# The long convolution of a hybrid encoder rewritten from radix four to radix eight

## The chip, the cores and the metric

The kernel is one program on one core of a Trainium2 chip, all in fp32 (the matmuls work on high and low parts, see below). The metric is the device time of one launch in microseconds (us), as the median of several runs. The engines have the names of the profile: PE is TensorE (PEld its weight loads), DVE is VectorE, ACT is ScalarE, POOL is GpSimd, SP is SyncE, which issues most DMAs.

## What is computed

Two encoder layers over 1024 tokens of width 1024. Each layer has token mixing, a cross-attention and a mixture of experts. Token mixing is a grouped-query attention, a long convolution ("hyena") of 256 channels and a latent attention, joined by one output projection. The change touches the convolution alone:

```python
def bidir_long_conv(z, h, bias):
    n_tok, c = z.shape[1], z.shape[2]
    hf, hb = h[:, 0], h[:, 1]
    filt_circ = jnp.concatenate([hf, jnp.zeros((1, c), jnp.float32), hb[1:][::-1]], axis=0)
    zf = z.astype(jnp.float32)
    zs = jnp.fft.rfft(zf, n=2 * n_tok, axis=1)
    fs = jnp.fft.rfft(filt_circ, axis=0)
    y = jnp.fft.irfft(zs * fs[None], n=2 * n_tok, axis=1)[:, :n_tok]
    return (y + zf * bias.astype(jnp.float32)).astype(z.dtype)

    # in hybrid_mix
    filt = hyena_filters(n_tok, hy_w1, hy_b1, hy_w2, hy_b2, hy_w3, hy_b3, hy_wout, hy_freq, hy_decay)
    out_b = x0 * bidir_long_conv(hv * x1, filt, hy_bias)
```

The filter h is the output of a small network (f3 in the kernel) times a decaying exponential, a window; it does not depend on x, and both layers' filters are transformed at the start of the program.

## The kernel before

**Transforms.** A transform of length 2048 with odd frequencies is split by the token index modulo four. Each of the four residues r has 256 tokens and a cosine and a sine table of 256 x 256. mm3 multiplies two operands that are each split in a high and a low part by three matmuls (L185 to L187); split (L173, L174) makes the two parts, the high one on ACT, the low one on DVE or POOL. dft_step does one residue: per kind (cosine, sine), per half of the frequencies and per half of the tokens an mm3 over 256 channels, 24 matmuls of 256 columns, the table stationary. evac (L179, L181) copies the result out of PSUM, on DVE and ACT in turn. Sums and differences of the residues ("butterflies") then give the spectrum F.

**filter_spectra** works both layers in three parts. First, per residue and layer, two windows: two matmuls (L868, L869), a product on DVE (L871), the sum and the difference of both halves on POOL (L875, L876), a split into pmh (ACT) and pml (DVE). Second, twelve dft_steps (the odd residues twice, since there sum and difference need both tables). Third, the butterflies (L916) and radix (L929), each one on DVE or POOL in turn by alt(); SP writes F to DRAM (fd). It is a generator, "fill": each next(fill) issues it up to its next yield. Two yields are taken in an earlier loop, 20 in the loop `for n in range(20)` (here the **filter loop**), beside the transposes of x and the projection's first tiles, and 22 in the **latent loop** of in_proj: for each of eight token tiles, 24 matmuls of 416 columns into one of two PSUM buffers (psO), with up to four next(fill) among them, and after them the tile's normalisation on ACT (square, root) and DVE (L371, L373, rotary L500 to L508), which frees the buffer.

**hyena(l)** is a generator as well. side() pulls it once per iteration of the attention, in iterations 3 to 57 except where n % 5 == 4 (44 pulls), and drains it at 58; one pull more comes before. It transposes z (L956), makes the four residues' transforms, does all butterflies on POOL, multiplies Z with F on POOL (L978 to L984), does the butterflies of the inverse on POOL (L990) and DVE (ab, L1004 to L1010), splits each ab (abh on ACT, abl on POOL) and transforms back with the spectrum stationary and the table moving. L1029 (DVE) adds the bias term from PSUM, into a buffer "yz", and L1033 (POOL) multiplies with the gate into mix.

**Attention** runs 96 iterations a layer, two to a head pair, of which the scores S (L524), the row maximum (DVE, L527), the exponential E (ACT, L533), four transposes (L541), the split of the probabilities (ACT PH, DVE PL) and the product with V (L551, L552) form a pipeline three iterations deep; S, T and O have two PSUM buffers each. After each pair put() moves the output: three copies on ACT (L563 to L565) into "olo", two instructions on POOL (L566, L567). olo and yz share one ring of two buffers:

```python
lo = self.tp.tile([128, 3, 256], F32, tag="olo", name="olo", bufs=2)       # put
t = self.tp.tile([128, 3, 256], F32, tag="olo", name="yz", bufs=2)[:, 0]   # hyena
```

**Order.** PE, ACT and DVE run in the order of the code; POOL's and SP's order is set by a scheduler at build time.

Of the kernel before, what the change touches and what calls it, by code (L numbers as in the profile page):

```python
# [19 lines left out]
D = 1024  # L20
# [47 lines left out]


# [14 lines left out]
def shape_constants():  # L84
# [10 lines left out]
    perm = np.concatenate([np.arange(r, N, 4) for r in range(4)])  # L95
# [6 lines left out]
    m, k = np.arange(256), np.arange(256)  # L102
    fwd, inv = [], []
    for r in range(4):
        th = np.pi * np.outer(4 * m + r, 2 * k + 1) / 2048
        cs = np.stack([np.cos(th), np.sin(th)], 1)
        fwd.append(cs.reshape(2, 128, 2, 256).transpose(1, 0, 2, 3).reshape(128, 1024))
        ci = (cs / 1024).transpose(2, 1, 0)
        inv.append(ci.reshape(2, 128, 2, 256).transpose(1, 0, 2, 3).reshape(128, 1024))
    for nm, v in (("k_dft", fwd), ("k_idft", inv)):  # L110
        v = np.stack(v).astype(np.float32)
        h = (v.view(np.uint32) + np.uint32(0x7FF) + ((v.view(np.uint32) >> np.uint32(12)) & np.uint32(1))) & np.uint32(0xFFFFF000)
        h = h.view(np.float32)
        out[nm] = np.stack([h, v - h], 1)
# [21 lines left out]
class Net:  # L136
# [661 lines left out]
    def table(self, name, r):  # L798
        res = []
        for i in range(2):  # L800
            t = self.big((128, 2, 2, 256), F32R, name="tab")
            self.nc.gpsimd.dma_start(t, self.A[name][r, i].rearrange("p (m c k) -> p m c k", m=2, c=2))
            res.append(t)
        return res

    def dft_step(self, r, tabs, cH, cL, sH, sL, free=False):

        nc = self.nc
        th, tl = tabs
# [6 lines left out]
        X = self.big((128, 2, 2, 256), name="X")  # L816
        if free:
            nc.scalar.activation(X, P, AF.Copy)
        else:
            self.evac(X, P)  # L820
        return X

# [4 lines left out]
    def filter_spectra(self):  # L827
# [13 lines left out]
        nc.sync.dma_start(tneg, A["k_tneg"])  # L841
        nxt = [self.table("k_dft", 0)]
# [4 lines left out]
        for w in ws:  # L847
            hl = self.big((128, 2, 512), F32R, name="woh")
            self.split(hl[:, 0], hl[:, 1], w)
            wp.append(hl)  # L850
        es, ends = {}, []

        def decay(j):
            if j < 8:
                r, l = divmod(j, 2)
                es[j] = []
                for i in (r * 2, r * 2 + 1):
                    e = self.tmp(name="win")
                    nc.scalar.activation(e, decs[l], AF.Exp, scale=tneg[:, i:i + 1])
                    es[j].append(e)  # L860

        def window(j, H, L):
            r, l = divmod(j, 2)
            a = slice(l * 64, l * 64 + 64)
            for mt in range(2):
                i = r * 2 + mt
                P, c = self.psO(), slice(i * 128, i * 128 + 128)
                nc.tensor.matmul(P, self.f3[l][:, c], wp[l][:, 0], start=True, stop=False)  # L868
                nc.tensor.matmul(P, self.f3[l][a, c], wp[l][a, 1], start=False, stop=True)  # L869
                e = es[j][mt]  # L870
                nc.vector.tensor_tensor(e, e, P, OP.mult)  # L871
                if i == 0:
                    nc.vector.memset(e[0:1, 256:512], 0.0)
                pm = self.tmp((128, 2, 256), name="pm")
                nc.gpsimd.tensor_tensor(pm[:, 0], e[:, 0:256], e[:, 256:512], OP.add)  # L875
                nc.gpsimd.tensor_tensor(pm[:, 1], e[:, 0:256], e[:, 256:512], OP.subtract)  # L876
                ends.append((H[:, :, mt, :], L[:, :, mt, :], pm))
            del es[j]

        def parts(n):  # L880
            for _ in range(n):
                self.split(*ends.pop(0))

        decay(0)
        yield
        G, H = [[], []], [{}, {}]
        for r in range(5):
            pms = []
            for l in range(DEPTH):
                if r < 4:  # L890
                    pmh = self.big((128, 2, 2, 256), F32R, name="pmh")
                    pml = self.big((128, 2, 2, 256), F32R, name="pml")
                    window(r * 2 + l, pmh, pml)
                    parts(len(ends) - 2)
                    decay(r * 2 + l + 1)
                    pms.append(((pmh[:, 0], pml[:, 0]), (pmh[:, 1], pml[:, 1])))
                    yield
                elif l == 0:
                    parts(2)
                if r > 0:  # L900
                    p, m = was[l]
                    G[l].append(self.dft_step(r - 1, tabs, *p, *m))
                    yield
                    if r % 2 == 0:
# [1032 lines left out]
```

## Time and profile before

| what | value |
|---|---|
| runs | 2755.35, 2754.78, 2750.19 us, median 2754.78 |
| profiled execution | 2756.29 us, span 2754.4 us |
| busy share of the span | PE 93%, PEld 79%, DVE 71%, ACT 57%, POOL 29% |
| chain that ended last | PE 72%, DVE 14%, ACT 5%, issue 5%, DMA 3%, POOL 1% |

The span is what the profiler sees of the execution; the rest of its time lies around it. Busy shares are means over the whole program, in which the convolution is a small part, so the stretches in which its pieces run have to be read by themselves: the filter loop at 83 to 143 us, the latent loop at 143 to 184, and two attentions, of which the first layer's has its iterations 15 to 48 at 422 to 517. In a row, `L916 POOL ... bf<-X 128x1024 x2` is two instructions of line 916 on POOL that make tile bf from tile X, 128 partitions by 1024 elements; the bracket at the end is the idle time of the engine before it and what ended that.

### The profile page before, as it was taken

To read this page: it belongs to the slowest core of one execution; us is meant where nothing else is said; L and a number is where in the kernel's file an instruction comes from. 1 tells how busy PE (TensorE), PEld (TensorE's weight loads), DVE (VectorE), ACT (ScalarE), POOL (GpSimd) and SP (SyncE) were. 2 spreads that over 40 slices of the span, in tenths; PEclk is the share of its full clock that TensorE was granted. 3 is DMA by queue.
4 is the path that set the end of the run, shared out by engine and by line. 5 is a ranking of instruction groups with operands and counts; after the bars stand their busy time and mean duration, and the time that the engine had idled before them with its cause. 6 is when DMAs were issued, how large, how long until landed. Compare 5 with 4: busy or idle time off the path is not lost.

```text
span 2754.4 us, 39814 instructions
## 1 busy us (share of the span) xinstructions
PE 2570.7 (93%) x14484; PEld 2175.1 (79%) x14484; DVE 1952.1 (71%) x3041; ACT 1577.6 (57%) x2804; POOL 810.4 (29%) x767
## 2 busy tenths in 40 slices
PE   7999989999999995999989999999999999599997
PEld 5788879888778884777869887988977888477775
DVE  6765568877653578889876556887765347888887
ACT  4633359878313443888854425887842344378885
POOL 3443427742201301111131333684230130011112
PEclk9999999999999997999999999999999999799999
DMA  7546110233232357999975611034223234799994
GB/s 194 183 163 206 40 47 32 93 100 96 81 99 86 104 180 256 348 378 371 342 238 170 211 62 47 24 100 100 72 90 107 77 101 175 248 329 371 378 345 153
DMA packets 224565, 468.04 MB, mean 170 GB/s; under 512 B 27001, under 2 KB 83919, under 8 KB 224368
## 3 DMA queue, kind: packets, MB, share of 16 engines
q1 hardware_dynamic: 197504, 369.32, 38.5%
q0 software_dynamic: 22256, 79.40, 10.4%
q10 hardware_dynamic: 4608, 16.78, 1.5%
q8 instruction: 114, 1.87, 0.3%
q14 instruction: 83, 0.68, 0.1%
HBM read 378.66 MB, written 86.77 MB: 169 GB/s over the span
## 4 chain that ended last, share of the span: by engine, by line
PE 72%; DVE 14%; ACT 5%; issue 5%; DMA 3%; POOL 1%; SPq 0%; ACTq 0%; DVEq 0%; POOLq 0%
PE S L185 8%; PE S L186 8%; PE S L187 7%; PE S L524 6%; PE O L1614 6%; PE T L541 5%; PE O L185 5%; PE O L186 5%; PE O L187 5%; PE S L418 4%; PE O L552 3%; PE O L551 3%; DVE rk L1417 1%; PE T L1368 1%; DMA ed<-moe_w_down 1%
## 5 line engine op out<-in xcount | busy, mean ns | idle before, releaser
L174 DVE TENSOR_TENSOR egl<-eg,egh 128x1024 fp32r<-128x1024 f32 x256 | 305.6, 1220 | 49.6 <-ACT egh L173 45.3
L527 DVE TENSOR_REDUCE nm<-S 128x1 f32<-128x1024 f32 x192 | 234.1, 1221 | 97.1 <-PE S L524 96.2
L173 ACT ACTIVATE egh<-eg 128x1024 fp32r<-128x1024 f32 x256 | 265.1, 1058 | 40.3 <-PE S L186 23.5
L174 DVE TENSOR_TENSOR PL<-T,PH 128x512 fp32r<-128x512 f32 x384 | 246.1, 682 | 17.3 <-ACT PH L173 15.0
L173 ACT ACTIVATE PH<-T 128x512 fp32r<-128x512 f32 x384 | 210.1, 595 | 81.7 <-PE T L541 80.4
L533 ACT ACTIVATE E<-S,nm 128x1024 f32<-128x1024 f32 x192 | 214.7, 1118 | 11.5 <-DVE nm L527 9.9
L185 PE MATMUL S<-woh,mh 128*128 128x512 f32 x512 | 207.8, 406 | 6.3 <-DVE r L1106 6.3
L541 PE MATMUL T<-ident,E 128*128 128x128 f32 x1536 | 206.1, 276 | 6.1 <-DVE PL L174 5.1
L541 PEld LDWEIGHTS T<-ident,E 128*128 128x128 f32 x1536 | 179.6, 142 | 40.1 <-DVE PL L174 14.6
L186 PE MATMUL S<-wol,mh 128*128 128x512 f32 x512 | 201.8, 394 | 2.8 <-POOL wol L174 2.4
L185 PE MATMUL S<-egh,xt 128*128 128x512 f32 x512 | 203.9, 398 | 0.0
L187 PE MATMUL S<-woh,ml 128*128 128x512 f32 x512 | 200.8, 392 | 0.0
L187 PE MATMUL S<-egh,xt 128*128 128x512 f32 x512 | 200.4, 391 | 0.0
L186 PE MATMUL S<-egl,xt 128*128 128x512 f32 x512 | 200.4, 391 | 0.0
L174 DVE TENSOR_TENSOR edl<-ed,edh 128x1024 fp32r<-128x1024 f32 x128 | 153.1, 1220 | 18.5 <-ACT edh L173 18.5
L1614 PE MATMUL O<-edh,ht 128*128 128x512 f32 x512 | 156.2, 408 | 1.4 <-ACT ht L173 1.4
L566 POOL TENSOR_TENSOR olo<-olo 64x256 f32<-64x256 f32 x96 | 70.2, 731 | 293.3 <-ACT olo L564 289.4
L524 PE MATMUL S<-KS,QS 128*128 128x512 f32 x512 | 148.2, 413 | 2.4 <-ACT E L533 2.4
L173 ACT ACTIVATE edh<-ed 128x1024 fp32r<-128x1024 f32 x128 | 132.4, 1055 | 22.9 <-PE S L186 13.2
L1556 POOL DMA_INDIRECT xg<-x2d,ix x32 | 54.9, 1715 | 299.2 <-PE O L1614 124.3
L551 PE MATMUL O<-PH,VS 128*128 128x256 f32 x512 | 138.6, 303 | 0.0
L552 PE MATMUL O<-PL,VS 128*128 128x256 f32 x512 | 127.9, 283 | 0.0
(409 smaller groups left out, 7127.1 us busy)
## 6 DMA issues: line engine op xcount, KB each, us to landing
eg<-moe_w_gate SPq DMA_DIRECT2D x128, 512.0 KB, 10.6
eg<-moe_w_up SPq DMA_DIRECT2D x128, 512.0 KB, 10.8
ed<-moe_w_down SPq DMA_DIRECT2D x128, 512.0 KB, 11.1
tab<-k_dft POOLq DMA_DIRECT2D x24, 512.0 KB, 4.6
wv<-xa_wkv SPq DMA_DIRECT2D x16, 512.0 KB, 7.7
wk<-xa_wkv SPq DMA_DIRECT2D x16, 512.0 KB, 6.6
tab<-k_idft POOLq DMA_DIRECT2D x16, 512.0 KB, 4.5
wo<-w_o SPq DMA_DIRECT2D x16, 512.0 KB, 3.5
```

Source lines behind the costliest of these rows:

```text
L173: self.nc.scalar.activation(h, src, AF.Copy)
L174: (self.nc.vector if le == "v" else self.nc.gpsimd).tensor_sub(l, src, h.bitcast(F32))
L185: mm(out, ah, bh, start=start, stop=False)
L186: mm(out, ah, bl, start=False, stop=False)
L187: mm(out, al, bh, start=False, stop=stop)
L524: self.nc.tensor.matmul(S[:, hf * 512:hf * 512 + 512], a, b[hf], start=n == 0, stop=n == len(passes) - 1)
L527: self.nc.vector.tensor_reduce(nm, S, axis=AX.X, op=OP.max, negate=True)
L533: self.nc.scalar.activation(E, S, AF.Exp, bias=nm, scale=1.0, accum_out=den)
L541: self.nc.tensor.transpose(pt[:, k, :], P[:, kt * 128:(kt + 1) * 128], self.ident)
L551: nc.tensor.matmul(O[:, :256], v, PH[half][:, k, :], start=kt == 0, stop=False)
L552: nc.tensor.matmul(O[:, :256], v, PL[half][:, k, :], start=False, stop=kt == 7)
L1614: nc.tensor.matmul(O[e][n], a[:, 2 * u + f, :], w[:, n * 512:n * 512 + 512], start=s, stop=z)
```

## The change

The split is by the token index modulo eight: eight residues of 128 tokens, tables of 128 x 128, two residues in one step. In the filter one stationary table meets a moving operand of 512 columns (sum and difference side by side), so one mm3 serves both; residues 0 and 4 need half of it. Each step's results go out as U on ACT and V on DVE. The butterflies have a level more, with two products of sqrt(1/2), done by ACT on a tile Q. In hyena, the inverse has the table stationary and the spectrum moving; its result, tokens on partitions, is copied out by ACT (yt), transposed by PE and multiplied with the gate by DVE out of PSUM. The bias is added to the filter's first tap, so zx (hv * x1) is not loaded again. side() pulls in every iteration from 3 to 57, and the filter loop pulls twice for n < 12 (32 yields there, 26 in the latent loop). The core of the diff:

```diff
-        P = self.psS((128, 2, 2, 256))
-        for cs, (xh, xl) in enumerate(((cH, cL), (sH, sL))):
-            for kt in range(2):
-                for mt in range(2):
-                    a = slice(kt * 128, kt * 128 + 128)
-                    self.mm3(P[:, cs, kt, :], th[:, mt, cs, a], tl[:, mt, cs, a], xh[:, mt, :], xl[:, mt, :], mt == 0, mt == 1)
...
+        def dft(r, l, i, tab, hl, U, V):
+
+            P = self.psS((128, 4, 256))
+            both = r % 4 > 0
+            for cs in range(2):
+                d = slice(0, 512) if both else slice(cs * 256, cs * 256 + 256)
+                o = P[:, cs * 2:cs * 2 + 2, :].rearrange("p a c -> p (a c)")[:, d]
+                self.mm3(o, tab[:, 0, i, cs, :], tab[:, 1, i, cs, :], hl[:, 0, d], hl[:, 1, d], True, True)
+            nc.scalar.activation(U, P[:, 0::3, :], AF.Copy)
+            if both:
+                nc.vector.tensor_copy(V, P[:, 1:3, :])
...
+            for k, (o, a, b, op) in enumerate((
+                    (E, u[0], u[1], OP.add), (O, u[2], u[3], OP.add), (Od, u[2], u[3], OP.subtract),
+                    (Oe, v[1], v[2], OP.add), (Dd, v[1], v[2], OP.subtract),
+                    (D[:, 0], u[0][:, 0], u[1][:, 0], OP.subtract), (D[:, 1], v[0][:, 0], v[0][:, 1], OP.subtract),
+                    (Q[:, 0], Od[:, 0], Od[:, 1], OP.subtract), (Q[:, 1], Dd[:, 0], Dd[:, 1], OP.add))):
                 self.alt().tensor_tensor(o, a, b, op)
-                yield
+                if k in (1, 3, 5, 8):
+                    yield
...
+    def radix(self, F, E, O, b2, D, Q, pool=False):
+        nc = self.nc
+        tt = lambda *x: (nc.gpsimd if pool else self.alt()).tensor_tensor(*x)
+        nc.scalar.activation(Q, Q, AF.Copy, scale=math.sqrt(0.5))
+        S, AB = (self.big((128, 2, 2, 256), name="bf") for _ in range(2))
+        tt(S[:, 0], E[:, 0], E[:, 1], OP.add)
+        tt(S[:, 1], O[:, 0], O[:, 1], OP.add)
+        yield
+        tt(AB[:, 0], E[:, 0], E[:, 1], OP.subtract)
+        tt(AB[:, 1], *b2, OP.subtract)
+        yield
+        tt(F[0][:, 0], S[:, 0], S[:, 1], OP.add)
+        tt(F[0][:, 1], S[:, 0], S[:, 1], OP.subtract)
+        yield
+        tt(E, D, Q, OP.add)
+        yield
+        tt(O, D, Q, OP.subtract)
+        yield
+        for f, x in zip(F[1:], (AB, E, O)):
+            for i, op in enumerate((OP.add, OP.subtract)):
+                tt(f[:, i], x[:, 0], x[:, 1, ::-1], op)
             yield
...
-                            self.mm3(P[:, ct, :], ah[:, cs, kt, a], al[:, cs, kt, a], th[:, kt, cs, :], tl[:, kt, cs, :], n == 0, n == 3)
-                            n += 1
-                for ct in range(2):
-                    t = self.tp.tile([128, 3, 256], F32, tag="olo", name="yz", bufs=2)[:, 0]
-                    nc.vector.scalar_tensor_tensor(t, zv[ct][:, q, :], hb[:, ct:ct + 1], P[:, ct, :], op0=OP.mult, op1=OP.add)
...
+                        dst = self.mix[hf][2][:, ct, :].rearrange("p (m r) -> p r m", r=8)[:, w, :]
+                        nc.vector.tensor_tensor(dst, p, zv[ct][:, w, s], OP.mult)
...
+                for i in range(2):
+                    for cs in range(2):
+                        k = (i, cs) if q == 0 else (i ^ cs, cs)
+                        self.mm3(P[:, i, :], tab[:, 0, i, cs, :], tab[:, 1, i, cs, :], ah[:, k[0], k[1], :], al[:, k[0], k[1], :], cs == 0, cs == 1)
+                t = self.tmp((128, 2, 256), name="yt")
+                nc.scalar.activation(t, P, AF.Copy)
+                late.append((q, t))
                 yield
...
             next(fill)
+            if n < 12:
+                next(fill)
...
-                if HY0 <= n < 58 and n % 5 != 4:
+                if HY0 <= n < 58:
                     next(hy, None)
```

POOL's butterflies of both layers' filters, which run in the latent loop; before (X is what the transforms left, bf and F are made here):

```order
L916 TENSOR_TENSOR bf<-X 128x1024 x2
L929 TENSOR_TENSOR F<-bf 128x1024
L929 TENSOR_TENSOR F<-bf 128x512 x2
L916 TENSOR_TENSOR bf<-X 128x1024 x2
L929 TENSOR_TENSOR F<-bf 128x1024
L929 TENSOR_TENSOR F<-bf 128x512 x2
```

and in the changed kernel, where the lines have the numbers of the new file:

```order
L916 TENSOR_TENSOR bf<-X 128x1024 x2
L916 TENSOR_TENSOR bf<-X 128x512
L916 TENSOR_TENSOR bf<-bf 128x512
L931 TENSOR_TENSOR bf<-bf 128x512 x2
L931 TENSOR_TENSOR bf<-bf 128x1024
L931 TENSOR_TENSOR F<-bf 128x512 x4
L916 TENSOR_TENSOR bf<-X 128x1024 x3
L916 TENSOR_TENSOR bf<-X 128x512
L916 TENSOR_TENSOR bf<-bf 128x512
L931 TENSOR_TENSOR bf<-bf 128x512 x2
L931 TENSOR_TENSOR F<-bf 128x512
L931 TENSOR_TENSOR bf<-bf 128x1024
L931 TENSOR_TENSOR F<-bf 128x512 x3
```

Six instructions of 1024 and four of 512 become seven and sixteen, in the same place. DVE has as many, between the normalisations; its last ones in the changed kernel, around the normalisation of the sixth tile (the second of the two that stand here; ri to cn):

```order
L373 RECIPROCAL ri<-sd 128x2
L375 SCALAR_TENSOR_TENSOR cn<-O,ri,mgq 128x256
L375 SCALAR_TENSOR_TENSOR cn<-O,ri,mgk 128x128
L502 TENSOR_TENSOR r_1509<-O,rope_368 128x32
L508 TENSOR_TENSOR r_1511<-O,rope_368 128x2x8 x2
L510 TENSOR_TENSOR cn<-r_1509,r_1511 128x32
L931 TENSOR_TENSOR bf<-bf 128x1024
L931 TENSOR_TENSOR F<-bf 128x512 x2
L373 RECIPROCAL ri<-sd 128x2
L375 SCALAR_TENSOR_TENSOR cn<-O,ri,mgq 128x256
L375 SCALAR_TENSOR_TENSOR cn<-O,ri,mgk 128x128
L502 TENSOR_TENSOR r_1559<-O,rope_368 128x32
```

Before, DVE's last butterflies stood behind the fourth tile's normalisation; now one of 512 stands behind the sixth's. ACT in the attention, from the E of iteration 40 on, before:

```order
L533 ACTIVATE E,den<-S,nm 128x1024
L173 ACTIVATE PH<-T 128x4x128 x2
L533 ACTIVATE E,den<-S,nm 128x1024
L563 ACTIVATE olo<-O 64x256
L564 ACTIVATE olo<-O 64x256
L565 ACTIVATE olo<-O 64x256
L173 ACTIVATE PH<-T 128x4x128 x2
```

and in the changed kernel:

```order
L535 ACTIVATE E,den<-S,nm 128x1024
L932 ACTIVATE bf<-bf 128x1024
L175 ACTIVATE PH<-T 128x4x128 x2
L535 ACTIVATE E,den<-S,nm 128x1024
L565 ACTIVATE olo<-O 64x256
L566 ACTIVATE olo<-O 64x256
L567 ACTIVATE olo<-O 64x256
L175 ACTIVATE PH<-T 128x4x128 x2
```

L932 is the scaling of the inverse's Q, whose two halves POOL makes; it stands ahead of the next split PH and the next E.

## Rows read from the trace of the kernel before

**Rows 1.** Engine busy time by stretch: filter loop, latent loop, middle of attention (columns in the prediction).

```profile
83.00:143.30 60.30, 57.84 (x383) 49.32 (x384) 44.95 (x59) 33.88 (x55) 31.97 (x39) 0.94 0.43 151
143.30:184.40 41.10, 38.20 (x194) 37.13 (x193) 32.52 (x62) 12.64 (x46) 24.37 (x11) 0.96 0.55 193
420.00:512.00 92.00, 92.00 (x675) 84.73 (x675) 80.46 (x114) 85.49 (x178) 79.27 (x65) 1.00 0.14 47
```

**Rows 2.** Timeline of TensorE in attention: start, length, engine, line, what.

```profile
382.28 0.28 PE L186 MATMUL S<-zt,tab 128*128 128x256 f32 x1
382.40 0.28 PE L187 MATMUL S<-zt,tab 128*128 128x256 f32 x1
```

**Rows 3.** Chain that ended last, early stretch: start, length, what.

```profile
195.97 2.76 PE S L418 x12
```

**Rows 4.** Groups by line and form, whole kernel, TensorE on the filter's tables.

```profile
L185 PE MATMUL S<-pmh,tab 128*128 128x256 f32 x96 | 29.1, 303 | 0.0
```

**Rows 5.** Groups by line and form in the filter loop, VectorE: count, busy, mean ns.

```profile
L174 DVE TENSOR_TENSOR pml<-pm,pmh 128x512 fp32r<-128x512 f32 x16 | 15.5, 1000 | 0.1
L871 DVE TENSOR_TENSOR win<-win,O 128x512 f32<-128x512 f32 x16 | 10.3, 677 | 1.7 <-ACT win L859 1.4 <-PE O L869 0.2
...
L179 DVE COPY X<-S 128x1024 f32<-128x1024 f32 x6 | 7.3, 1216 | 0.4 <-PE S L187 0.4
```

**Rows 6.** The same view of the filter loop, POOL.

```profile
L876 POOL TENSOR_TENSOR pm<-win 128x256 f32<-128x256 f32 x16 | 14.9, 929 | 0.0
```

**Rows 7.** Waits in the filter loop: total us, times, longest.

```profile
ACT win L859 <- POOL pm L876: 12.9, 8, 2.4
```

**Rows 8.** Timeline of POOL in attention.

```profile
488.45 2.39 POOL L978 TENSOR_TENSOR y<-Z,F 128x1024 f32<-128x1024 f32 x1
490.81 1.29 POOL L980 TENSOR_TENSOR y<-Z,F 128x512 f32<-128x512 f32 x1
...
507.58 0.73 POOL L566 TENSOR_TENSOR olo<-olo 64x256 f32<-64x256 f32 x1
...
509.21 2.40 POOL L990 TENSOR_TENSOR bf<-y,y 128x1024 f32<-128x1024 f32 x1
```

**Rows 9.** Timeline of VectorE in the latent loop.

```profile
156.97 2.34 DVE L508 TENSOR_TENSOR cn<-r,r 128x32 f32<-128x32 f32 x1
...
162.09 1.21 DVE L916 TENSOR_TENSOR bf<-X 128x1024 f32<-128x1024 f32 x1
...
170.50 1.28 DVE L929 TENSOR_TENSOR F<-bf 128x512 f32<-128x512 f32 x2
...
173.65 0.19 DVE L508 TENSOR_TENSOR cn<-r,r 128x32 f32<-128x32 f32 x1
```

**Rows 10.** Timeline of POOL in the latent loop.

```profile
143.00 6.52 POOL L916 TENSOR_TENSOR bf<-X 128x1024 f32<-128x1024 f32 x2 [11.44 <-PE S L187]
```

**Rows 11.** Timeline of TensorE in the latent loop, with the idle time before.

```profile
161.31 0.35 PE L186 MATMUL O<-wil,xh 128*128 128x416 f32 x1
161.50 0.35 PE L187 MATMUL O<-wih,xl 128*128 128x416 f32 x1
164.63 0.69 PE L185 MATMUL O<-wih,xh 128*128 128x416 f32 x1 [2.78 <-DVE r L506]
...
165.46 0.55 PE L187 MATMUL O<-wih,xl 128*128 128x416 f32 x1
165.81 0.55 PE L185 MATMUL O<-wih,xh 128*128 128x416 f32 x1
```

**Rows 12.** Timeline of ACT in attention, first layer.

```profile
422.00 1.11 ACT L533 ACTIVATE E<-S,nm 128x1024 f32<-128x1024 f32 x1
...
516.88 1.12 ACT L533 ACTIVATE E<-S,nm 128x1024 f32<-128x1024 f32 x1
...
562.95 0.38 ACT L563 ACTIVATE olo<-O 64x256 f32<-64x256 f32 x1 [8.12 <-POOL mix L1033]
...
564.84 1.11 ACT L533 ACTIVATE E<-S,nm 128x1024 f32<-128x1024 f32 x1
```

More of the change, by code (lines that the diff above doesn't have):

```diff
@@ L850, in filter_spectra @@
             wp.append(hl)
+        order = [(r, l) for st in FWD for r in st for l in range(DEPTH)]
         es, ends = {}, []
         def decay(j):
[L854 to L863, printed above, removed]
-            a = slice(l * 64, l * 64 + 64)
[L865 to L878, printed above, removed]
@@ L880, in parts @@
         def parts(n):
-            for _ in range(n):
+            while len(ends) > n:
                 self.split(*ends.pop(0))
+        def dft(r, l, i, tab, hl, U, V):
[8 more added lines that the diff above has]
+                nc.vector.tensor_copy(V, P[:, 1:3, :])
@@ L884, in filter_spectra @@
         decay(0)
         yield
-        G, H = [[], []], [{}, {}]
-        for r in range(5):
-            pms = []
-            for l in range(DEPTH):
[L890 to L896, printed above, removed]
+        sh = (128, 2, 2, 256)
@@ L897, in filter_spectra @@
+        U, V = [[], []], [[], []]
+        old = []
+        for n in range(9):
+            new = []
+            for l in range(DEPTH):
+                if n < 8:
+                    new.append(window(2 * n + l))
+                    parts(1)
+                    decay(2 * n + l + 1)
                     yield
                 elif l == 0:
[L899 to L902, printed above, removed]
-                    yield
-                    if r % 2 == 0:
-                        H[l][r - 1] = self.dft_step(r - 1, tabs, *m, *p)
-                        yield
@@ L907, in filter_spectra @@
[L907 to L920 removed]
+                    parts(0)
@@ new lines, in filter_spectra @@
+                if n > 0:
+                    r, i = order[2 * n - 2][0], (n - 1) % 2
+                    if i == 0:
+                        U[l].append(self.big(sh, name="X"))
+                    if r in (2, 1, 5):
+                        V[l].append(self.big(sh, name="X"))
+                    dft(r, l, i, tab, old[l], U[l][-1][:, i], V[l][-1][:, int(r in (6, 3, 7))] if r % 4 else None)
+                    yield
+            old = new
+            if n % 2 == 0 and n < 8:
+                tab = nxt.pop()
+                if n < 6:
+                    nxt.append(self.table("k_dft", n // 2 + 1))
@@ new lines, in hyena @@
+        E, O, D, Od, Q = (self.big(sh, name="bf") for _ in range(5))
+        for i, j in ((0, 0), (1, 1)):
+            tt(E[:, j], Y[i][:, 0], Y[i][:, 1], OP.add)
+            tt(D[:, j], Y[i][:, i], Y[i][:, 1 - i], OP.subtract)
+            yield
+        tt(O, Y[2], Y[3], OP.add)
+        yield
+        tt(Od, Y[2], Y[3], OP.subtract)
+        yield
+        tt(Q[:, 0], Od[:, 0], Od[:, 1], OP.add)
+        tt(Q[:, 1], Od[:, 1], Od[:, 0], OP.subtract)
+        del Y
+        yield
+        G = [self.big(sh, name="G") for _ in range(4)]
@@ new lines, in hyena @@
+            if 0 < n < 5:
+                q, ah, al, tab = ready.pop(0)
+                P = self.psO((128, 2, 256))
+                for i in range(2):
+                    for cs in range(2):
+                        k = (i, cs) if q == 0 else (i ^ cs, cs)
[3 more added lines that the diff above has]
+                late.append((q, t))
```

210 lines of the change are left out of this document (105 added, 105 removed).

## Prediction

> **What bounds the kernel now.** I read the kernel in the three stretches that the change touches, first by the table of engine busy time per stretch [rows 1], whose columns give the length of a stretch and then what each engine was busy in it. In the filter loop (83.0 to 143.3 us of the span) TensorE works 57.84 of 60.30 us, and VectorE 44.95. In the input projection's latent loop (143.3 to 184.4) TensorE works 38.20 of 41.10. In the middle of attention (420 to 512) it works all 92.00, with ACT at 85.49 and POOL at 79.27. So TensorE sets the pace in each, but in attention POOL has only 13 us of 92 to spare, and it is POOL that the change loads. Then I read single rows: what a matmul of each width costs, and how VectorE and POOL behave when both run butterflies. A row's start is its second place to look: the distance between starts is what an instruction costs its engine, its own length is a little more.
>
> **The change part by part.** All sums are made against the profiled execution, 2756.3 us, which lies 1.5 above the median of 2754.8.
>
> Matmuls. A 256-column matmul follows the one before it after 0.12 us [rows 2]; twelve of 512 columns take 2.76, 0.23 each [rows 3]. The filter has 3 x 96 = 288 of the narrow kind (one of its three lines stands in [rows 4]) in twelve steps of 24; each hyena has four such steps forward, 96, and as many in the inverse. After: the filter has 72 wide and 24 narrow ones, 72 x 0.23 + 24 x 0.12 = 19.4 against 288 x 0.12 = 34.6, so 15.2 us less; each hyena 48 and 48, so 5.8 less in each direction.
>
> Filter loop. Taking 15.2 from TensorE's 57.84 leaves 42.6, and VectorE is next: its six evacuations of 1024 (7.3 us in all) become twelve of 512 (0.64 each, as 10.3 / 16 of the window's product) [rows 5], so 44.95 - 7.3 + 7.7 = 45.4. If VectorE alone bounds the loop with the same 2.5 us of gaps as TensorE had, it lasts 47.9: -12.4. But the four steps of a window hang together: product with the window on VectorE 0.68, sum and difference on POOL 2 x 0.93, the low part on VectorE 1.00 [rows 5, 6], 3.54 for each of 16, or 56.6 if none of it overlaps the next window. That ACT's decay already waits 12.9 us for POOL's difference [rows 7] says that this ring of buffers is tight, so I take the end near it, -4, with -12 and 0 as bounds. The load of the bias row and one add on a single partition are two small instructions beside sixteen windows, and go for nothing. Half as many table loads are issued; no wait for a table stands among this stage's waits.
>
> Latent loop. The butterflies of both layers are pulled here, and they double: before, POOL and VectorE each have 6 of 1024 and 4 of 512; after, each has 7 and 16, and ACT scales two tiles. On POOL one of 1024 costs 2.36, from its start to the next, 0.03 less than its length, and so one of 512 1.26 [rows 8]; on VectorE, undisturbed, 1.21 and 0.64 [rows 9]. Worked one after the other, before is 6 x 2.36 + 4 x 1.26 + 6 x 1.21 + 4 x 0.64 = 29.0 us. The trace shows the first at 143.00 [rows 10] and the last VectorE pair ending at 171.78 [rows 9], 28.8 in all, with no overlap left. That the two engines keep each other out is also seen in a single row: the 32-element sum of L508 took 2.34 while POOL ran, and 0.19 at 173.65 when it didn't [rows 9].
>
> The Trainium skill, in "SBUF — State Buffer", section "Who interferes with whom", says why: a VectorE instruction with two inputs in SBUF and a GpSimd instruction that reads SBUF take the same port, and the later one blocks for the whole of the earlier. That trace agrees (0.19 against 2.34). By the rule the doubled butterflies cost this loop what is worked out below; if they ran side by side they would cost it nothing. The rule also exempts a VectorE instruction with one input in PSUM, and the trace agrees: of two products of 128 x 512 in the filter loop the one with an input in PSUM took 677 ns and the one without 1000 [rows 5].
>
> After, in series: 7 x 2.36 + 16 x 1.26 + 7 x 1.21 + 16 x 0.64 = 55.4 us, more than the loop's 41.1. VectorE's order is written out and holds the normalisation of each token tile between the butterflies; an accumulator is free, and TensorE may start the tile after next, only behind it. One such wait is there already: TensorE idle 2.78 for r of L506, at 164.63 [rows 11]. In the new order the normalisation of the sixth tile stands behind all butterflies but a last one on VectorE and POOL's last three, 55.4 - 0.64 - 3 x 1.26 = 51 us in; the eighth tile's 24 matmuls at 0.19 [rows 11] are 4.6 more, its own normalisation about 1: 57, or **+16**. Bounds: 0 if POOL's 36.7 runs beside VectorE's share; +22 if the last tile waits for all 55.4 and runs its matmuls at the 0.35 that lies between two starts after that wait [rows 11], 8.4.
>
> Attention, the end of hyena. The iteration (the E activations) runs at (516.88 - 422.00)/33 = 2.875 us [rows 12]. The last eleven before the drain take 564.84 - 516.88 = 47.96, 16.3 over eleven such; 11.5 of it is the inverse's 96 matmuls (0.12 each), and a single wait of 8.12, ACT's first put copy behind POOL's L1033 [rows 12], covers the rest and more. The two are in one ring of two buffers ("olo"); the new code takes the inverse's tile from another ring, so the wait goes. After: 48 x 0.12 = 5.8, 16 transposes of half the width, at most 0.12 each, 1.9, and 1 for what waits remain: 8.7, so -7.6. The 5.8 of the forward transform is gained too: it lies in iterations where POOL has nothing of hyena to do. Together **-13.4** a layer.
>
> Attention, POOL. All butterflies and products are POOL's. In the new order POOL's first one stands behind the put pair of iteration 11, and ACT's second scaling of Q behind the E of iteration 40. Counted from the E of iteration 10, POOL can start when that E (1.1) and the put's three copies (0.38 each at most [rows 12]) are done, at 2.2; up to Q it has 12 of 1024, 36 of 512 and 15 put pairs, 509.21 - 507.58 = 1.63 each [rows 8]: 28.3 + 45.4 + 24.5 = 98.2, so Q is there at 100.4. ACT gets to the scaling at 30 x 2.875 + 1.1 = 87.4 and waits 13.0; behind it on ACT stand the splits of the probabilities and the next E, and TensorE waits for both, though its two score buffers let it be one iteration (2.9) ahead. From there to the first split of the inverse, eight iterations on, POOL needs 2 x 2.36 + 12 x 1.26 + 4 x 1.63 = 26.4 against 8 x 2.875 = 23.0: 3.4 more. Together 16.4 without cover, 10.6 if an iteration is hidden each time; I take **+13**, midway, since ACT at 85 of 92 us wins back little in between. The four "ab" additions that leave VectorE, the 16 products L1033 that move from POOL to VectorE, and ACT's copies of the transposed tile fall behind iteration 47, where POOL and VectorE have room; taken at nothing, inside the 1 us above. Of the table loads, which POOL issues, the forward ones stand ahead of its first butterfly and the first inverse one just ahead of the first split of the inverse, where six stood; on SP four reloads remain of six; no table or reload is waited for in the trace of these iterations, so none of it has a price.
>
> Sum: -4 + 16 + 2 x (13 - 13.4) = **+11**: 2767 for the profiled execution, 2766 against the median.
>
> **The rivals.**
> (a) The butterflies run beside each other, or TensorE doesn't feel them: the latent loop costs 0. The sum is -4 + 0 - 1 = -5, 2750. Against it stand the 28.8 against 29.0; for it, that only part of VectorE's order lies on TensorE's path.
> (b) On the other side: POOL's lag never reaches ACT. Place: the second scaling of Q. Price: 13 per layer. It decides if POOL is done with Q by 87.4 + 2.9 us, that is if its instructions cost a tenth less than the rows say, or if ACT wins back enough between the waits that TensorE never lacks an E. Sum -4 + 16 - 26.8 = -15: 2740. For it: POOL's work before fitted without any wait by TensorE. Against it: 98 us don't go into 87 or 90.
> (c) Both (a) and (b): all TensorE time saved is earned, -4 - 26.8 = -31, 2724.
> (d) Everything at its full price: the filter loop 0, the latent loop +22, the lag 16.4: 0 + 22 + 2 x 3.0 = +28, 2783.
>
> **How the numbers follow.** Forecast 0.48 (its own range 2757 to 2774), (a) 0.17, (b) 0.15, (c) 0.08, (d) 0.12. Within 0.2%, or 5.5 us, about what a measurement of this kernel can tell from no change, lie most of (a), 0.12, and the low edge of the forecast, 0.06. Faster: (b), (c) and the rest of (a), 0.28. Slower: 0.42 of the forecast and (d), 0.54. The range leaves out (c) and the outer halves of (b) and (d): 2738 to 2783.
>
> **What would show it.** In the changed profile: the filter loop some 4 us shorter, with VectorE and not TensorE its busiest engine; the latent loop near 57 us long, TensorE idle before L185 with VectorE named as what ended it, and butterflies of 1024 on VectorE longer than 1.21; in attention ACT idle some 10 us before the second scaling of Q, POOL named, and no 8 us wait before the put near iteration 58. I am wrong if the latent loop stays near 41 us, or if the iterations 10 to 48 still run at 2.875.

## The result

The changed kernel takes 2770.98 us (median of 5 runs, 2770.18 to 2772.47), the kernel before 2755.35 (5 runs). The ratio is 1.0055, 95% interval 1.0039 to 1.0071: 15.6 us slower. The forecast was 2766 with 2738 to 2783 around it. The profiled executions have spans of 2768.7 and 2754.4, 14.3 apart, and the 14.3 can be laid out by place. A place is from one mark in the trace to the same mark in the other (first window's matmul, first and last matmul of the latent loop, the first E of each attention):

| place | before | after | difference | forecast |
|---|---|---|---|---|
| up to the first window's matmul | 81.47 | 80.50 | -1.0 | 0 |
| filter loop | 61.6 | 54.5 | -7.1 | -4 |
| latent loop, to the start of its last matmul | 41.0 | 59.9 | +18.9 | +16 |
| from there to the first E | 176.2 | 176.1 | -0.1 | 0 |
| attention of the first layer, E of 0 to E of 95 | 321.6 | 323.7 | +2.0 | -0.4 |
| attention of the second layer | 321.7 | 323.4 | +1.7 | -0.4 |

What lies between and behind the attentions is equal within 0.1. The stretches of the changed kernel in the view that [rows 1] come from (length, then busy time of PE, PEld, DVE, ACT, POOL, then the granted clock of TensorE; filter loop, latent loop, two pieces of the first attention):

```profile
80.50:135.00 54.50, 46.81 (x194) 31.64 (x193) 41.53 (x66) 37.66 (x67) 29.69 (x35) 0.87 0.43 148
135.00:195.20 60.20, 45.14 (x195) 42.07 (x195) 53.24 (x76) 14.81 (x49) 46.22 (x24) 0.86 0.38 129
425.70:498.70 73.00, 71.78 (x525) 65.66 (x525) 62.24 (x89) 67.18 (x139) 71.36 (x62) 1.00 0.09 30
498.70:531.00 32.30, 25.33 (x171) 22.70 (x170) 19.89 (x29) 22.24 (x47) 31.36 (x27) 0.89 0.10 33
```

In the latent loop POOL went from 24.37 to 46.22 us of work and VectorE from 32.52 to 53.24, and TensorE, with the same matmuls, from 38.20 to 45.14: its clock fell from 0.96 of full speed to 0.86. VectorE in the latent loop (start, length, engine, line, what), the rows that answer to [rows 9]:

```profile
139.79 3.67 DVE L916 TENSOR_TENSOR bf<-X 128x1024 f32<-128x1024 f32 x3
145.72 0.69 DVE L916 TENSOR_TENSOR bf<-X 128x512 f32<-128x512 f32 x1 [2.25 <-POOL bf L916]
...
150.41 4.58 DVE L931 TENSOR_TENSOR bf<-bf 128x512 f32<-128x512 f32 x2
...
157.89 1.21 DVE L510 TENSOR_TENSOR cn<-r,r 128x32 f32<-128x32 f32 x1
...
167.48 7.34 DVE L916 TENSOR_TENSOR bf<-X 128x1024 f32<-128x1024 f32 x3
...
188.87 0.68 DVE L931 TENSOR_TENSOR F<-bf 128x512 f32<-128x512 f32 x1
...
190.76 0.19 DVE L510 TENSOR_TENSOR cn<-r,r 128x32 f32<-128x32 f32 x1
```

Two instructions of 512, worth 1.28, took 4.58; two of 1024 with one of 512, worth 3.1, took 7.34; the 32-element L510 took 1.21 beside POOL's butterflies and 0.19 behind the last of them. From the first butterfly to the last is 139.79 to 189.55, 49.8 us, where 55.4 were forecast. TensorE in the same loop, answering to [rows 11]:

```profile
149.41 0.69 PE L187 MATMUL O<-wih,xh 128*128 128x416 f32 x1 [4.93 <-DVE r L508]
149.90 0.55 PE L188 MATMUL O<-wil,xh 128*128 128x416 f32 x1
150.24 0.55 PE L189 MATMUL O<-wih,xl 128*128 128x416 f32 x1
...
158.00 0.42 PE L187 MATMUL O<-wih,xh 128*128 128x416 f32 x1 [1.07 <-DVE r L508]
158.27 0.35 PE L188 MATMUL O<-wil,xh 128*128 128x416 f32 x1
158.46 0.35 PE L189 MATMUL O<-wih,xl 128*128 128x416 f32 x1
...
166.62 0.69 PE L187 MATMUL O<-wih,xh 128*128 128x416 f32 x1 [3.82 <-DVE r L508]
...
176.15 0.43 PE L187 MATMUL O<-wih,xh 128*128 128x416 f32 x1 [2.08 <-DVE r L508]
...
182.07 0.43 PE L187 MATMUL O<-wih,xh 128*128 128x416 f32 x1 [1.15 <-DVE r L508]
...
188.87 0.42 PE L187 MATMUL O<-wih,xh 128*128 128x416 f32 x1 [2.01 <-DVE r L508]
...
190.15 0.55 PE L189 MATMUL O<-wih,xl 128*128 128x416 f32 x1
190.50 0.55 PE L187 MATMUL O<-wih,xh 128*128 128x416 f32 x1
```

It waited six times, 15.1 us in all, for the rotary that frees a PSUM buffer (once, 2.78, before), which is 12.3 more. The rest of the 18.9 is its slower matmuls: behind the waits of 4.93, 3.82 and 2.01 us they start 0.35 apart for 3 to 6 us, behind the other three 0.19 apart. VectorE, for which it waits, has no gap from 145.72 until behind the last normalisation. ACT in the first attention, answering to [rows 12]; L932 is the scaling of Q, L565 a put's first copy:

```profile
425.71 1.11 ACT L535 ACTIVATE E<-S,nm 128x1024 f32<-128x1024 f32 x1
...
430.32 1.06 ACT L932 ACTIVATE bf<-bf 128x1024 f32<-128x1024 f32 x1 [0.80 <-POOL bf L997]
...
502.17 0.38 ACT L565 ACTIVATE olo<-O 64x256 f32<-64x256 f32 x1 [2.27 <-POOL mix L569]
...
510.99 1.06 ACT L932 ACTIVATE bf<-bf 128x1024 f32<-128x1024 f32 x1 [5.58 <-POOL bf L1032]
...
530.97 1.12 ACT L535 ACTIVATE E<-S,nm 128x1024 f32<-128x1024 f32 x1
...
576.82 1.11 ACT L535 ACTIVATE E<-S,nm 128x1024 f32<-128x1024 f32 x1
```

From the E of iteration 15 (425.71) to that of 48 (530.97) are 105.26 us; before it was 94.88 [rows 12]. The three waits are for POOL: 0.80 at the first scaling, 2.27 when the ring of the put is full, 5.58 at the second scaling. TensorE stood still behind them (the transposes of E):

```profile
433.83 1.25 PE L543 MATMUL T<-ident,E 128*128 128x128 f32 x8 [1.22 <-DVE PL L176]
...
504.66 1.26 PE L543 MATMUL T<-ident,E 128*128 128x128 f32 x8 [1.68 <-DVE PL L176]
...
513.31 1.97 PE L543 MATMUL T<-ident,E 128*128 128x128 f32 x8 [5.29 <-DVE PL L176]
```

POOL itself had no gap in all that time: one row before its first butterfly, and the first gap after it (start 548.90):

```profile
413.59 0.73 POOL L568 TENSOR_TENSOR olo<-olo 64x256 f32<-64x256 f32 x1 [7.74 <-ACT olo L566]
...
548.90 2.37 POOL L176 TENSOR_TENSOR abl<-G,abh 128x1024 fp32r<-128x1024 f32 x1 [2.26 <-ACT abh L175]
```

### The profile page after: what moved, and what is told of

Read it like the earlier page. It is cut to its first block, busy times and chain, and to the rows that moved or that the text cites. A ratio compares the mean times of both kernels' runs of the same rounds, so it can differ in the third digit from the quotient of the medians.

```text
span 2768.7 us, 39154 instructions
## 1 busy us (share of the span) xinstructions
PE 2548.5 (92%) x14132; PEld 2146.8 (78%) x14132; DVE 1960.4 (71%) x3066; ACT 1588.1 (57%) x2828; POOL 872.8 (32%) x784
## 3 DMA queue, kind: packets, MB, share of 16 engines
q1 hardware_dynamic: 196386, 367.22, 37.9%
## 5 line engine op out<-in xcount | busy, mean ns | idle before, releaser
L176 DVE TENSOR_TENSOR PL<-T,PH 128x512 fp32r<-128x512 f32 x384 | 246.2, 683 | 40.5 <-ACT PH L175 38.2
L1673 POOL DMA_INDIRECT yd<-ye,ix x31 | 49.0, 1582 | 260.8 <-DVE egl L176 114.0
```

The source lines that it names most:

```text
L176: (self.nc.vector if le == "v" else self.nc.gpsimd).tensor_sub(l, src, h.bitcast(F32))
```

## The experiments

A median is given with its ratio to the kernel before, from runs on the same chip. Where a stretch is compared, it is taken from the traces, since the medians of the kernel before lie between 2753.0 and 2755.4 on the chips used.

**Butterflies of the filters on one engine.** alt() gives VectorE only:

```diff
-        return self.nc.vector if self.flip else self.nc.gpsimd
+        return self.nc.vector
```

> The changed kernel with all butterflies of the filters on VectorE, none on POOL. Theory (the two engines exclude each other, so what counts is the sum of both shares): VectorE's share becomes 14 x 1.21 + 32 x 0.64 = 37 us instead of 18.7 + 36.7 in series; with eight normalisations of 1.3 us between them the latent loop goes from 60 us to about 50, so 8 to 12 us less than the changed kernel's 2771, and no L510 longer than 0.2 us. Rival (it is VectorE's own order that TensorE waits for, POOL runs beside it): VectorE gets 18 us more and the loop lengthens by 5 to 15 us.

2761.8 us, ratio 1.0024 (1.0014 to 1.0033), 9.2 below the changed kernel. The latent loop took 50 us instead of 60, with POOL idle. VectorE (same view as above):

```profile
139.53 7.21 DVE L916 TENSOR_TENSOR bf<-X 128x1024 f32<-128x1024 f32 x7
...
149.17 0.19 DVE L510 TENSOR_TENSOR cn<-r,r 128x32 f32<-128x32 f32 x1
149.28 2.49 DVE L931 TENSOR_TENSOR bf<-bf 128x512 f32<-128x512 f32 x4
```

The first seven (five of 1024 and two of 512, worth 7.3 undisturbed) took 7.21, four of 512 2.49, and no L510 is longer than 0.19. So one engine alone is faster than the two in turns: halving the work gained nothing, because the halves ran one after the other. That the exclusion is the cause and not VectorE's order is shown by the sign: VectorE got more to do, and the loop became shorter.

**Fewer butterflies in the latent loop.**

```diff
             for k in range(0, 8, 2):
                 go(wl, P[:, :416], t, (k, k + 1))
-                next(fill, None)
+                if l or k % 4 == 0:
+                    next(fill, None)
...
-                if n == NT - 1 + (l > 0):
-                    drain(mem if l else fill)
+                if l and n == NT:
+                    drain(mem)
+                if not l and n >= 6:
+                    for _ in range(2):
+                        next(fill, None)
+                if not l and n == 12:
+                    drain(fill)
```

> The changed kernel with the filters' butterflies pulled more slowly: two pulls per token tile in the latent loop instead of four, the other ten in the later part of the input projection. About the same number of butterfly microseconds as before the change (29) then falls in the latent loop. Theory (what the latent loop lost, 19 us, is the series of both engines' butterflies, longer than the loop): the loop goes back to 41 to 48 us, and the rest is mostly hidden in the 176 us behind it, where VectorE works 93 and POOL 66: 8 to 17 us less than 2771. Rival (the loss comes from the tables, evacuations or buffers of the new form, whatever the place of the butterflies): less than 4 us.

2764.0, ratio 1.0037 (1.0023 to 1.0051): only 7 gained. The latent loop did go back to 41 us (136.9 to 177.5), so its loss is the amount of butterflies in it, as expected; but the stretch behind it, 176 us before, grew by 12.6. There ACT waits for Q, and then for a weight (start, length, engine, line, what, then the idle time before):

```profile
183.70 1.06 ACT L933 ACTIVATE bf<-bf 128x1024 f32<-128x1024 f32 x1 [8.90 <-DVE bf L917]
...
195.14 0.84 ACT L175 ACTIVATE uqh<-uq 128x768 fp32r<-128x768 f32 x1 [4.09 <-DMA uq<-mla_w_uq]
```

SP issued the load of uq at 188.69, 11 us after the loop's last matmul; before, at 183.34, just ahead of it. The trace shows what stood ahead of it: SP waited 8.7 us to load mgq (start 186.84), for VectorE's normalisation (L376), and uq came behind that; in the kernel before and in the changed one uq stands ahead of mgq. Another order on SP wasn't tried.

**The ring of the put, in the kernel before.**

```diff
-                    t = self.tp.tile([128, 3, 256], F32, tag="olo", name="yz", bufs=2)[:, 0]
+                    t = self.tmp(name="yz")[:, :256]
```

> The kernel before, with yz taken from another ring than the put's olo, nothing else changed. Theory of the prediction (the wait of 8.12 us before the put's copy is a loss by itself): 6 to 8 us less per layer, 12 to 16 below before. Rival (the wait stands in the place of another: the put or the E behind it would wait for the inverse's matmuls and products anyway): 0 to 6 us in all.

2751.9, ratio 0.9995 (0.9986 to 1.0005). By the trace iterations 49 to 58 went from 43.9 to 42.5 us in the first layer and from 45.3 to 42.5 in the second: 1.4 and 2.9, not 6 to 8. Iteration 58, which has the long wait and in which side() drains the rest of hyena, only went from 11.22 to 9.94. Most of the wait of 8.12 thus stood in the place of others and was no price. These ten iterations then take as long as in the changed kernel (42.6), which has half the matmuls there.

**The copy yt, one pull later.**

```diff
         for n in range(6):
+            if late:
+                q, P = late.pop()
+                t = self.tmp((128, 2, 256), name="yt")
+                nc.scalar.activation(t, P, AF.Copy)
+                late.append((q, t))
...
-                t = self.tmp((128, 2, 256), name="yt")
-                nc.scalar.activation(t, P, AF.Copy)
-                late.append((q, t))
+                late.append((q, P))
```

> The changed kernel, with ACT's copy of the inverse's result (yt) issued one pull later, behind the next E, instead of right behind the matmuls that it waits for. In the changed kernel ACT stands idle 1.3 to 1.8 us before each of the four copies of a layer, 5.9 in all. Theory (these waits are why the end of hyena gained only some 2 us a layer where 7.6 were expected): 3 to 5 us less per layer, 6 to 10 in all. Rival (TensorE's own work and POOL's low parts pace these iterations, the waits are slack): less than 2 us in all.

2778.1, ratio 1.0086 (1.0070 to 1.0103): 7 us more. Iterations 49 to 58 went from 42.6 to 45.8 us (44.7 in the second layer); TensorE's transposes now wait for the copy. A view of waits of that stretch (total us, times, longest):

```profile
PE T L1062 <- DVE PL L176: 3.4, 2, 1.7
...
PE T L1062 <- ACT yt L1046: 2.5, 2, 1.4
```

**The copy yt on VectorE.**

```diff
-                nc.scalar.activation(t, P, AF.Copy)
+                nc.vector.tensor_copy(t, P)
```

> The changed kernel with the copy yt of the inverse's result on VectorE instead of ACT, at the same place. The late copy cost 3 us a layer instead of gaining, since the transpose waited for it. Theory (ACT, busy 33 of 43 us there with 10 us of waits in its order, is what paces iterations 49 to 58): with 2.4 us of copies and 5.9 us of waits off ACT these ten iterations take 1 to 4 us less, 2 to 8 in all. Rival (the chain matmul, copy, transpose, product through the attention's own PSUM buffers paces them, whichever engine copies): within 1.5 us either way.

2770.4, ratio 1.0050 (1.0033 to 1.0067); iterations 49 to 58 at 42.4 instead of 42.6. The rival holds: which engine copies doesn't matter, and ACT's waits there were slack.

**Less work for POOL.** The products' cross terms are left out (the second sum takes operands that are there):

```diff
-            tt(t2[:, :, 0], z[:, :, 0], F[:, d, 1], OP.mult)
-            tt(t2[:, :, 1], z[:, d, 1], F[:, :, 0], OP.mult)
...
-            tt(y[:, :, 1], t2[:, :, 0], t2[:, :, 1], OP.add)
+            tt(y[:, :, 1], t1[:, :, 0], z2, OP.add)
```

> The changed kernel with part of hyena's products left out: the eight cross products of 512 a layer (t2) aren't made, and the sum that used them takes other operands, so the output is not the convolution. POOL has 8 x 1.25 = 10 us less to do per layer, everything else has the same number of instructions. Theory (in iterations 16 to 48 POOL's queue is the bound, and ACT's wait before the second scaling is where that shows): the wait of 7.9 us there goes, iterations 16 to 48 take 92 to 95 us instead of 102.7, 8 to 10 us less per layer, 16 to 20 in all. Rival (the loss comes from the change's extra instructions on ACT and the order on it, not from POOL's amount of work): less than 5 us in all.

2757.9, ratio 1.0010 (1.0001 to 1.0020), 13 below the changed kernel. Iterations 16 to 48 take 93.6 us (102.7 in the changed kernel), and the wait before the second scaling is gone: POOL's amount of work is the cause. But iterations 49 to 58 grew from 42.6 to 46.8 (45.4 in the second layer). Ahead of the inverse's first matmul:

```profile
533.82 0.55 PE L187 MATMUL O<-abh,tab 128*128 128x256 f32 x1 [4.01 <-DMA tab<-k_idft]
```

This is the inverse's first table, which POOL issues just ahead of the first low part. Fewer products don't take POOL's lag away behind iteration 48: the issue stands 9.0 us behind the E of 48 here (529.71 against 520.72) and 7.6 in the changed kernel (538.61 against 530.97), where TensorE waits 2.56 at the same matmul. What the second scaling no longer shows is seen here in part.

**The scaling folded away.**

```diff
-        nc.scalar.activation(Q, Q, AF.Copy, scale=math.sqrt(0.5))
...
-        tt(E, D, Q, OP.add)
+        nc.vector.scalar_tensor_tensor(E, Q, math.sqrt(0.5), D, op0=OP.mult, op1=OP.add)
         yield
-        tt(O, D, Q, OP.subtract)
+        nc.vector.scalar_tensor_tensor(O, Q, -math.sqrt(0.5), D, op0=OP.mult, op1=OP.add)
```

(in hyena only; the filters keep the scaling)

> The changed kernel without ACT's two scalings of Q in each hyena: the factor goes into the two instructions behind it (D + cQ, D - cQ), which move from POOL to VectorE as one scalar-tensor-tensor each, four of 1024 a layer. POOL gets 9.4 us less, VectorE 4 x 1.21 more, each of which may wait for a POOL instruction or block one. Theory (POOL is the bound and ACT's place in the order makes TensorE feel it): most of the 10 us of iterations 16 to 48 comes back, 6 to 10 us a layer, 12 to 20 in all. Rival (the two engines' exclusion gives it back, VectorE's low parts come late and TensorE waits for them instead): 0 to 6 in all, or a loss.

2762.3, ratio 1.0022 (1.0013 to 1.0032), 8.7 below. The layers gain 4.5 and 4.0 us, between theory and rival. The wait moved to VectorE, and the exclusion shows on both sides (VectorE, then POOL, same columns):

```profile
512.19 2.27 DVE L948 SCALAR_TENSOR_TENSOR bf<-bf 128x1024 f32<-128x1024 f32 x1 [3.36 <-POOL bf L931]
...
516.71 2.67 DVE L948 SCALAR_TENSOR_TENSOR bf<-bf 128x1024 f32<-128x1024 f32 x1
```

```profile
513.34 1.70 POOL L568 TENSOR_TENSOR olo<-olo 64x256 f32<-64x256 f32 x1
```

VectorE waits 3.36 for POOL's sums of L931, then takes 2.27 for 1.3 us of work; a put instruction on POOL, 0.73 elsewhere, takes 1.70 beside it.

**All of it in one.** alt() on VectorE, the slower pulls, and the scaling folded in filters and hyena:

> All that the runs so far point to in one: butterflies of the filters on VectorE alone, two pulls per token tile in the latent loop and the other ten behind it, the scaling folded into D + cQ and D - cQ (on VectorE, in hyena too), nothing of it on ACT. Theory (series of the two engines, ACT's waits for Q, POOL's amount): latent loop 41 to 45 us with at most 4 us lost behind it, so -15 to -19 there; hyena -6 to -10 a layer: 2735 to 2745, below both kernels. Rival (the loss behind the latent loop that the slower pulls showed, 12.6 us, is VectorE's or the tables', and hyena's fold gives nothing): 2755 to 2765.

2749.9, ratio 0.9979 (0.9970 to 0.9989): below both kernels, between what theory and rival gave. The latent loop took 36.6 us, 23 less than in the changed kernel, and 13 of it were lost behind it: no ACT wait for Q is there any more, but one of 7.26 for the weight uq, which SP issued at 182.99, 11 us after the loop's end, again behind a load of mgq that waited 8.7.

**POOL's queue started earlier.** In the combined kernel, E and D are made as soon as the first two transforms are there, when POOL is idle:

```diff
                 X.append(x)
+                if n == 2:
+                    E, D = (self.big(sh, name="bf") for _ in range(2))
+                    nc.gpsimd.tensor_tensor(E, X[0], X[1], OP.add)
+                    nc.gpsimd.tensor_tensor(D, X[0], X[1], OP.subtract)
                 yield
...
+        yield
+        yield
         G = [self.big(sh, name="G") for _ in range(4)]
```

> The combined kernel (10), and in hyena the first two butterflies (E and D, which need the first two transforms only) are issued as soon as these are there, in iterations in which POOL is idle; the two pulls so saved are put as empty pulls ahead of the second scaled sums. Nothing is added or left out. Theory (POOL's queue from iteration 10 on is the bound of iterations 16 to 48, and its lag shows at the second D + cQ): 2 x 2.36 = 4.7 us less lag a layer, iterations 41 to 48 go from 26.4 to some 22 us, 3 to 5 us less a layer, 6 to 10 in all below the combined kernel: 2740 to 2744. Rival (the stall there is the exclusion of VectorE and POOL around the scaled sums, not the lag): within 2 us of 2750.

2740.7, ratio 0.9952 (0.9939 to 0.9964), 12 below the kernel before on the same chip and 30 below the changed one. Nothing is added or left out; 4.7 us of POOL's work only start earlier. From the E of iteration 40 to that of 48 it takes 25.7 us instead of 30.4 in the combined kernel, 4.7 less, but some of that is lost ahead of it: iterations 16 to 48 gain 4.1 us (3.9 in the second layer). The second scaled sums on VectorE in that kernel, without a wait ahead of them:

```profile
503.44 1.74 DVE L949 SCALAR_TENSOR_TENSOR bf<-bf 128x1024 f32<-128x1024 f32 x1
...
507.43 2.71 DVE L949 SCALAR_TENSOR_TENSOR bf<-bf 128x1024 f32<-128x1024 f32 x1
```

**The table loaded earlier.** As the last, with the inverse's first table loaded before the second butterflies:

> As the one before, and the first table of the inverse is loaded before the second set of butterflies instead of just ahead of the first low part. Theory (with POOL's lag gone, TensorE waits for that table, as in the kernel with fewer products, where it waited 4.0 us for it): 2 to 4 us a layer less than the one before. Rival (enough lag remains that the table is there in time): the same within 2 us.

2743.9, ratio 0.9964 (0.9952 to 0.9976): nothing gained, the rival holds. Iterations 49 to 58 take 40.5 us, as without it (40.6). In the kernel without this edit TensorE's wait for the table was only 0.54.

**Without the inverse's transposes.**

```diff
-                pt = self.psT((128, 2, 2, 128))
-                for i in range(2):
-                    for ct in range(2):
-                        nc.tensor.transpose(pt[:, i, ct, :], t[:, i, ct * 128:ct * 128 + 128], self.ident)
...
-                        p = pt[:, :, ct, s] if a < b else pt[:, ::-1, ct, s]
+                        p = t[:, :, ct * 128 + hf * 64:ct * 128 + hf * 64 + 64]
```

> The kernel with the early pair (12), with the 16 transposes of the inverse's result left out: VectorE's products with the gate take ACT's copy as it is (tokens on partitions), so the output is not the convolution. PSUM buffers of the attention's transposes are no longer borrowed. Theory (in iterations 49 to 58 the inverse's own turn through those buffers, and the waits of TensorE and VectorE around it, are why half the matmuls gained little): these ten iterations go from 40.6 us to 35 to 37.5, 3 to 5.5 us less a layer, more than the 1.9 us that the transposes cost by themselves. Rival (ACT's splits and copies pace them, or POOL's low parts): 39 to 40.6, at most 1.9 us less a layer.

2739.9, ratio 0.9950 (0.9934 to 0.9967). Iterations 49 to 58 take 37.9 us, 2.7 less: more than the transposes by themselves, less than the theory's 3. Neither is confirmed; the medians don't tell the two kernels apart.

## Why the prediction was right, and where it wasn't

**Direction and size came from the right place.** The latent loop was forecast as +16 and measured +18.9, from the mechanism named: the first run says that the two engines' shares add, the second that the amount of butterflies in the loop is the loss. Rival (a) falls. (Of the two rows of 128 x 512 that the prediction set side by side, the one of 1000 ns is a low part and not a product; the reading stays the same.) In the Trainium skill, "SBUF — State Buffer", section "Who interferes with whom", issue order decides who blocks; the traces agree on both sides (L510 1.21 against 0.19 on VectorE behind POOL's earlier butterflies in the changed kernel, a put 1.70 against 0.73 on POOL behind VectorE's earlier sum in the kernel with the folded scaling).

**Within that term errors offset each other.** The sixth tile's normalisation, which frees the buffer for the last tile, was forecast 51 us into the loop and TensorE got the buffer at 188.87, 53.9 us in. The series itself was priced at 55.4 us and took 49.8. One of POOL's 1024 had run before it, at 135.38, and VectorE's lengths were summed where the starts lie a little closer; some 2 us of the difference are open. But the forecast let the series begin with the loop, and VectorE's first butterfly stands behind two low parts and an evacuation, 4.8 us into it. The last tile's matmuls then took 6.0 us where 4.6 were forecast, since some of them ran at the lower clock, which only the upper bound had counted. Over the whole loop TensorE's busy time grew by 6.9 us for the same matmuls, at a granted clock of 0.86 (0.96 before); but in the earlier tiles this cost nothing, since TensorE waited for VectorE behind them, and VectorE had no gap.

**The filter loop, -4, measured -7.1.** Inside the bounds of -12 and 0. The price per window was 3.54, the loop's 54.5 us are 3.4 for each of 16. It was set against 60.3 us, but the loop before began at 81.47, not at 82.97, and so lasted 61.6; that is 1.3 of the 3 us missed. VectorE has 41.53 of 54.5 busy, so it doesn't bound the loop, against what the last part of the prediction said to look for; TensorE still is the busiest, at 46.81. Its busy time fell by 11 us where 15.2 were forecast, at a granted clock of 0.87 (0.94 before). Whether the chain of a window paces the loop, as the price assumed, wasn't tried, so that 3.4 lies so near 3.54 may be luck.

**Attention, forward: -5.8 a layer.** From the E of 0 to that of 16 the two layers gained 7.0 and 4.9. The difference lies in iteration 3 of the kernel before, which takes 7.64 us in one layer and 5.60 in the other; why is open.

**Attention, POOL's lag: +13, measured +10.4** between iterations 15 and 48 (105.26 against 94.88), 10.3 in the second layer, just under the lower end of 10.6. The mechanism, the place and the order of the waits hold: fewer products take 9.1 of the 10.4 away, and 4.7 us of POOL's work started earlier take 4.1 and 3.9 us off the combined kernel's iterations 16 to 48. Rival (b) falls. The size was a little too large. The prediction had ACT wait 13.0 at the second scaling; it waits at three places, 0.80 at the first scaling, 2.27 at the full ring of the put and 5.58 at the second scaling, with TensorE idle 1.22, 1.68 and 5.29 behind them. How much the score buffers hide at each wasn't measured.

**The end of hyena: -7.6, measured -2.1 and -4.3.** This is the step that failed, and it failed as the prediction put it: a wait of 8.12 us was taken for a loss of its own. Taken away in the kernel before, it gave 1.4 and 2.9 us. The sum of matmuls, 5.8 us less, was also counted as if TensorE set the pace in these iterations: over the eleven up to the drain the inverse was to cost 8.7 us, and it costs 14.2 (45.85 less eleven of 2.875). TensorE doesn't set it: in the kernel before with its own ring, and in the changed kernel, the ten iterations read (same columns as the stretches above)

```profile
517.00:559.50 42.50, 40.47 (x302) 37.12 (x303) 31.53 (x47) 30.09 (x59) 24.87 (x35) 1.00 0.28 85
```

```profile
534.20:576.80 42.60, 37.10 (x275) 33.73 (x274) 30.31 (x52) 32.73 (x64) 24.71 (x27) 1.00 0.31 85
```

TensorE works 40.47 of 42.50 and 37.10 of 42.60: what it saved it spent waiting. Part of that hangs on POOL's lag, at the inverse's first matmul:

```profile
542.62 0.36 PE L187 MATMUL O<-abh,tab 128*128 128x256 f32 x1 [2.56 <-ACT E L535]
```

The profile names ACT's E, which this matmul doesn't read; it starts 4.0 us behind POOL's issue of the table (538.61), as in the run with fewer products (4.1), so the table is the likelier cause, which isn't shown. With the scaling folded away the wait is 0.46, and the ten iterations take 40.5. A further 2.7 went with the transposes of the result and their turn through the attention's own PSUM buffers (in the kernel with the early pair). Which engine makes the copy is excluded. A rest of some 3 us over the iterations' 28.8 and the inverse's matmuls is open.

**Together.** That the result lies 5 us from the forecast owes something to errors of opposite sign: against the terms of the sum the filter loop with its start came out 4 lower, the latent loop 3 higher, POOL's lag 5 lower in both layers, the end of hyena 9 higher, and the iterations behind the drain, 59 to 95, 0.7 longer in each layer, which no step had; 0.5 of that lies in iteration 59 itself, and its cause is open.

## What to carry to other kernels

Fewer matmuls help only where TensorE sets the pace; before halving them, write down for each engine that takes over work how much room it has in that stretch, and put a slow engine's queue where it can start early, not only where its results are used. A consumer of a slow engine's result on an engine with a fixed order (ACT's scaling of Q) makes everything behind it wait: folding it into its successor gave 8.7 us here. Work dealt out in turns to VectorE and GpSimd with all inputs in SBUF may be faster on VectorE alone (here 9 us).

## What the hardware showed that was not expected

TensorE ran slower behind some of its waits, and the length of the wait alone doesn't tell behind which. In the latent loop the matmuls behind waits of 4.93, 3.82 and 2.01 us started 0.35 apart for 3 to 6 us, those behind 2.08, 1.15 and 1.07 us 0.19 apart. In the attention the stretch with the waits of 1.68 and 5.29 us had a granted clock of 0.89, where its neighbours had 1.00; only the matmuls behind the 5.29 were slower (256 columns 0.21 apart instead of 0.12). Not all of it cost time: of the 6.9 us that TensorE was busy longer in the latent loop, only some 1.5 lengthened it, at the last tile (6.0 us from its first start to its last, 4.4 in the tile at 176.15), since VectorE set the pace before. And a wait seen in a profile, long and with one cause (8.12 us, POOL's L1033), gave back a sixth of itself in one layer and a third in the other when its cause was removed.
